# Two-layer retention and attention encoder: the last head's mean square in one full-precision product, attention's output off two banks, gates in pieces

## The chip, the cores and the metric

The kernel runs on one core of a Trainium2 chip. The metric is the time of one execution on the device, in microseconds (us); less is better. The engines are TensorE (PE: matrix products, its weight loads shown as PEld), VectorE (DVE), ScalarE (ACT), GpSimd (POOL) and SyncE (SP, which issues most transfers). Products accumulate in PSUM, in banks; the other working data lie in SBUF.

## The reference

There are 272 tokens (256 and 16 learned ones), 1024 channels and two layers. A layer has a retention branch and a windowed attention branch side by side, merged by sigmoid gates, and then a squared-ReLU MLP.

```python
def retention_branch(q, k, v, gate, log_decay, pad):
    ...
    o = retention_dir(qc, kc, vc, log_decay[0], True) + flip(
        retention_dir(flip(qc), flip(kc), flip(vc), log_decay[1], False))
    o = o.transpose(0, 2, 3, 1, 4).reshape(B, Lp, RET_HEADS, RET_V_DIM)[:, pad:]
    mu = jnp.mean(o, axis=-1, keepdims=True)
    var = jnp.mean(jnp.square(o - mu), axis=-1, keepdims=True)
    o = (o - mu) * lax.rsqrt(var + EPS)
    o = o.reshape(B, L, RET_V).astype(gate.dtype)
    return o * jax.nn.silu(gate)

def reference(...):
    ...
    for l in range(DEPTH):                                   # DEPTH = 2
        u = rms_norm(h, norm_mix_pre[l])
        proj = u @ w_in[l]
        ...
        y_r = retention_branch(...) @ w_ret_o[l]
        y_a = attention_branch(...) @ w_att_o[l]
        mix = (jax.nn.sigmoid(gate_r) * y_r + jax.nn.sigmoid(gate_a) * y_a) @ w_mix_o[l]
        h = h + rms_norm(mix, norm_mix_post[l])
        u = rms_norm(h, norm_ff_pre[l])
        ff = jnp.square(jax.nn.relu(u @ w_ff1[l])) @ w_ff2[l]
        h = h + rms_norm(ff, norm_ff_post[l])
    return h[:, N_META:]
```

The change touches the normalization of retention's output (`rsqrt` of the mean square over a head's 128 channels), the two sigmoid gates, and the product with `w_att_o`.

## The kernel before

Activations lie transposed: 128 channels on the partitions, 272 tokens in the free dimension (256 in the second layer where `c0` is 16). Weights come as units of 128x1024 float32, each split by ACT (line 131, `wh`) and DVE (line 132, `wl`) into a high and a low part in fp32r, in a ring of four; a product is three matmuls per 128 input channels (`mm3`, lines 136 to 138), 24 per unit. PE runs its instructions in one order, and so do ACT and DVE; a scheduler sets these orders from what becomes ready when, within the limits that `tc.issue_after` (not before a named instruction) and `tc.keep_in_program_order` give.

Retention runs head by head (`similar`, `retained`, `normed`, lines 670 to 711). `retained` (line 689) makes a head's output `po` in a bank of tag o (even heads) or t (odd heads), and squares it on ACT; lines 696 and 697 split the square into two fp32r parts `sqs`, one by ACT, one by DVE. `normed` (line 699) takes their mean over the channels by two matmuls against a constant 1/128 (line 702), into a bank of tag t, and then ACT computes Ln (705), Exp with -0.5 (706) and a Square (163), which DVE refines by a Newton step, multiplies by the gate and by `po`, and splits into `rh` and `rl`, the input of the product `ret_o`. Between these steps `fill` puts the products of the units `gate_r` and `gate_a`, so that PE has work while a head's chain runs. The bank tags have 3 (a), 2 (s), 2 (t) and 1 (o) banks; `wide()` (line 85) deals tags a, s and t in turn.

ACT's functions come in sets of tables, and a set is loaded before a function that the present one lacks (ACT_TABLE_LOAD in the rows). Ln and Exp are both in `natural_log_exp_and_others`, Tanh is not. The kernel asks for this set by `preload_act_table_set` at lines 207, 650 and 743; the loads ahead of Tanh (lines 649 and 740) are put in when the program is built, as every load is that the source does not ask for. A sigmoid is computed by Tanh: for `g_r` at line 649, ahead of the heads, and for `gate_r` (`thr`, one instruction) and `gate_a` (`tha`, eight) at lines 740 to 742, held behind the last head's Exp. Then come the product `att_o` (lines 745 to 753), whose result is multiplied with the gate `tha`, `ret_o` (lines 756 to 761), `mix` with the norm behind it (`leave`, line 296, by `mean`, line 180, ten matmuls on zeros, `warm`, line 175, and `rsqrt`, line 186, an Ln, an Exp and a Square on ACT), and the MLP. `leave` runs after the mixer and the first layer's MLP, three times in all; `rsqrt` runs once more at line 378 for each layer's first norm. The last norm (`scaled`, line 834) has an Ln and an Exp for each half of the tokens.

Of the kernel before, what the change touches and what calls it, by code (L numbers as in the profile page):

```python
# [10 lines left out]
F32R = mybir.dt.float32r  # L11
F16 = mybir.dt.float16
BF16 = mybir.dt.bfloat16
AF = mybir.ActivationFunctionType
# [3 lines left out]
P = 128  # L18
# [4 lines left out]
T = SEQ + NM  # L23
# [18 lines left out]
def encoder(ctx: ExitStack, tc: tile.TileContext, order, w, h_in, gains, dec, decm, sink, sinkm, tabs, mats, esel, masks, rel, relm, grow, out):  # L42
    nc = tc.nc
    V, A, PE, G = nc.vector, nc.scalar, nc.tensor, nc.gpsimd
    mul, add, sub, mn = ALU.mult, ALU.add, ALU.subtract, ALU.min

    def pool(name, bufs=1, **kw):
        return ctx.enter_context(tc.tile_pool(name=name, bufs=bufs, **kw))
# [6 lines left out]
    four = pool("four", 4)  # L55
# [5 lines left out]
    def slot(i, name, shape=(KD, T), dt=F32):  # L61
        return big.tile([P] + list(shape), dt, tag=f"b{i}", name=name)
# [4 lines left out]
    def half(i, name):  # L67
        return rows(slot(i, name, (4, T)))

    def tokens(i, name, shape=(KD,), at=32):  # L70
        return slot(i, name, (*shape, ROW), F32R)[..., at:at + T]

    def bank(tag, shape=None):
        t = psum.tile([P, 512], F32, tag=tag, name="ps_" + tag, bufs=BANKS[tag])
        if shape is None:
            return t
        n = int(np.prod(shape))
        v = t[:, :n]
        if len(shape) == 2:
            v = v.rearrange("p (a b) -> p a b", a=shape[0])  # L80
        elif len(shape) == 3:
            v = v.rearrange("p (a b c) -> p a b c", a=shape[0], b=shape[1])
        return v

    def wide():
        turn[0] += 1
        return "asatats"[turn[0] % 7]

    def f(t):
        return t.bitcast(F32)  # L90

    def stt(o, a, s, b, op0=mul, op1=mul):
        V.scalar_tensor_tensor(out=o, in0=a, scalar=s, in1=b, op0=op0, op1=op1)

    def split(xh, xl, x):
        A.activation(xh, x, AF.Copy)  # L96
        V.tensor_tensor(out=xl, in0=x, in1=f(xh), op=sub)  # L97
# [37 lines left out]
    def mm3(ps, ah, al, bh, bl, first=True, last=True):  # L135
        PE.matmul(ps, ah, bh, start=first, stop=False)  # L136
        PE.matmul(ps, ah, bl, start=False, stop=False)  # L137
        return PE.matmul(ps, al, bh, start=False, stop=last)  # L138
# [18 lines left out]
    def proj(x, c0, tag, *name):  # L157
        for _, ps in product(x, c0, tag, *name):
            pass
        return ps  # L160

    def newton(y1, x, e, y, w2):
        sq = A.activation(w2, y, AF.Square)
        if e:
            stt(w2, x, e, w2, op0=add)
        else:
            V.tensor_tensor(out=w2, in0=x, in1=w2, op=mul)
        if y1 is not None:
            stt(y1, w2, 3.0, y, op0=sub)
        return sq  # L170
# [49 lines left out]
    def square(src, c0):  # L220
        sq = two.tile([P, T], F32, tag="sq", name="sq", bufs=3)
        A.activation(sq[:, c0:], src, AF.Square)
        return sq
# [101 lines left out]
    mat = {}  # L325
# [37 lines left out]
    for l in range(DEPTH):  # L363
        c0 = 16 * l
# [5 lines left out]
        if l == 0:  # L370
            mat_sb = load(mats, name="mats")
            mat.update((n, mat_sb[:, i]) for i, n in enumerate(MATS))
            o128 = one.tile([P, P], F32R, tag="o128", name="o128")
# [124 lines left out]
        ao = tokens(5, "ao", (2, 4), 32 - c0)  # L498
# [3 lines left out]
        thr = slot(6, "thr")  # L502
# [46 lines left out]
        def behind():  # L549
            return tc.issue_after(anchor[0])  # L550
# [12 lines left out]
        if l == 0:  # L563
            ps = bank("s")
# [86 lines left out]
        tha = gate["gate_a"] = half("10a", "tha")  # L651
# [16 lines left out]
        sds, pos, pvs = {}, {}, {}  # L668
# [20 lines left out]
        def retained(hh):  # L689
            t = hh // 2  # L690
            po = pos[hh] = bank("ot"[hh % 2], [T])
            for c in range(2):
                PE.matmul(po[:, c0:], vr[:, c, hh * P:(hh + 1) * P], sds[hh][c][:, c0:], start=c == 0, stop=False)
            PE.matmul(po[:, c0:], vm[:, hh], tm[:, t, c0:], start=False, stop=True)
            sq = square(po[:, c0:], c0)
            pvs[hh] = four.tile([P, 2, T], F32R, tag="pt", name="sqs", bufs=3)
            split(*(pvs[hh][:, i, c0:] for i in range(2)), sq[:, c0:])

        def normed(hh):
            pv = bank("t", [T])  # L700
            for i in range(2):
                PE.matmul(pv[:, c0:], o128, pvs[hh][:, i, c0:], start=i == 0, stop=i == 1)
            y = two.tile([P, T], F32, tag="t1", name="vy")
            w2 = two.tile([P, T], F32, tag="t2", name="vw")
            A.activation(y[:, c0:], pv[:, c0:], AF.Ln, bias=eps)
            last = A.activation(y[:, c0:], y[:, c0:], AF.Exp, scale=-0.5)
            newton(w2[:, c0:], pv[:, c0:], 1e-6, y[:, c0:], w2[:, c0:])
            stt(w2[:, c0:], w2[:, c0:], -0.25, gt[:, hh, c0:])
            V.tensor_tensor(out=w2[:, c0:], in0=pos[hh][:, c0:], in1=w2[:, c0:], op=mul)
            split(rh[:, hh, c0:], rl[:, hh, c0:], w2[:, c0:])  # L710
            return last
# [6 lines left out]
        for hh in range(8):  # L718
            with behind():
                if hh < 7:  # L720
                    similar(hh + 1)
                retained(hh)
            fill(F[7])
            if hh == 0:
                for m in range(KD):
                    with tc.issue_after(ready.ins):
                        stt(gt[:, m, c0:], tg[:, m, c0:], 1.0, gt[:, m, c0:], op0=add)
                rh, rl = tokens(7, "rh", at=32 - c0), tokens(8, "rl", at=32 - c0)
            if hh % 2 and hh < 7:
                with behind():  # L730
                    meta((hh + 1) // 2)
            fill(F[6])
            with behind():
                last = normed(hh)
            fill(F[5])
        while queue or current:
            fill(1)

        with tc.issue_after(last.ins):
            A.activation(thr[:, :, c0:], thr[:, :, c0:], AF.Tanh, scale=0.5)  # L740
            for x in tha:
                A.activation(x[:, c0:], x[:, c0:], AF.Tanh, scale=0.5)
        tc.keep_in_program_order(A.preload_act_table_set("natural_log_exp_and_others"))

        for m2 in range(4):
            wh, wl = unit("att_o", m2)
            for i in range(2):
                m = 2 * m2 + i
                ps = bank(wide(), [T])
                for k in range(4):  # L750
                    sl = slice((4 * i + k) * P, (4 * i + k + 1) * P)
                    mm3(ps[:, c0:], wh[:, sl], wl[:, sl], ao[:, 0, k, c0:], ao[:, 1, k, c0:], k == 0, k == 3)
                stt(tha[m][:, c0:], tha[m][:, c0:], 1.0, ps[:, c0:], op0=add)

        z = tokens(2, "zh", at=32 - c0), tokens(3, "zl", at=32 - c0)
        for m in range(KD):
            ps = proj((rh, rl), c0, wide(), "ret_o", m)
# [17 lines left out]
        fs, behind = [], []  # L775
# [8 lines left out]
        for m in range(KF):  # L784
# [4 lines left out]
            ps = proj(u, c0, wide(), "ff1", m)  # L789
# [54 lines left out]
    for j in range(2):  # L844
# [22 lines left out]
        for i in range(2):  # L867
            sl = slice(j * 512, (j + 1) * 512)
# [6 lines left out]
    for i in range(2):  # L875
        for a, b in ((0, 512), (512, 768), (768, 1024)) if i else ((0, 512), (512, 1024)):
            sl = slice(a, b)
# [115 lines left out]
```

## Time and profile before

| what | us |
| --- | --- |
| median of 3 runs (866.87 to 868.93) | 868.81 |
| the profiled execution, its own time | 874.68 |
| its span, first to last instruction | 872.9 |
| PE busy / ACT busy in it | 854.7 / 564.8 |
| first layer's heads in it | 131 to 190 |
| second layer's heads in it | 568 to 624 |

The page gives one profiled execution: busy time per engine, the chain of work that ended last, and groups of instructions with what ended the idle time before them. Times of steps below are from this execution, in us from the start of its span. A row of a timeline has the start, the duration, the engine, the line in the kernel, the operation, what it writes and reads, the size and a count; in brackets stands the engine's idle time before it and what ended it.

### The profile page before, as it was taken

The numbers are of one execution on the slowest core, as the hardware profiler recorded it, in microseconds if no ns is written. First come the engines' busy times: TensorE is split into PE (matmuls) and PEld (weight loads), VectorE is DVE, ScalarE is ACT, GpSimd is POOL, SyncE is SP. The second block draws the span as 40 slices with busy tenths as digits, with TensorE's granted clock in tenths as the row PEclk, the third lists the DMA queues.
The fourth block names the chain that finished last, engine by engine and source line by source line (L and its number), as shares of the span: only waits on it lengthen the run. The fifth ranks groups of instructions, "written<-read, shape, count | busy, mean of one in ns | idle before, by whom it ended". The sixth has DMA issues, their size and how long they took to land.

```text
span 872.9 us, 16696 instructions
## 1 busy us (share of the span) xinstructions
PE 854.7 (98%) x6514; PEld 822.2 (94%) x6514; DVE 608.5 (70%) x1129; ACT 564.8 (65%) x1050; POOL 50.6 (6%) x114
## 2 busy tenths in 40 slices
PE   9999999999999999999999999999999999999997
PEld 8899999999989999999989999999999999998885
DVE  7889888878668555444468898888786775554544
ACT  7448788675558777544455578987845587783432
POOL 2112220000000000000000122200000000000000
PEclk9999999999999999999999999999999999999999
DMA  8544443446545655655635544434376276666661
GB/s 293 194 125 139 122 130 114 145 146 192 164 128 179 190 179 178 176 184 172 178 112 153 162 132 141 141 124 148 115 219 200 90 239 189 183 193 194 190 192 70
DMA packets 41407, 142.15 MB, mean 163 GB/s; under 512 B 5360, under 2 KB 6256, under 8 KB 41328
## 3 DMA queue, kind: packets, MB, share of 16 engines
q1 hardware_dynamic: 40896, 140.43, 52.3%
q8 instruction: 51, 0.84, 0.4%
q10 hardware_dynamic: 432, 0.66, 0.2%
q14 instruction: 28, 0.23, 0.1%
HBM read 140.02 MB, written 1.05 MB: 162 GB/s over the span
## 4 chain that ended last, share of the span: by engine, by line
PE 80%; DVE 10%; ACT 6%; issue 1%; DMA 1%; POOL 0%; SPq 0%; DVEq 0%; ACTq 0%; POOLq 0%
PE ps_a L136 12%; PE ps_a L137 12%; PE ps_a L138 12%; PE ps_s L138 5%; PE ps_s L136 5%; PE ps_s L137 5%; PE ps_t L136 4%; PE ps_t L137 4%; PE ps_t L138 4%; DVE wl L132 3%; PE ps_s L853 2%; PE ps_a L853 2%; PE ps_a L855 2%; PE ps_s L855 2%; PE ps_s L854 2%; PE ps_a L854 2%
## 5 line engine op out<-in xcount | busy, mean ns | idle before, releaser
L132 DVE TENSOR_TENSOR wl<-raw,wh 128x1024 fp32r<-128x1024 f32 x256 | 313.0, 1224 | 199.7 <-ACT wh L131 198.2
L131 ACT ACTIVATE wh<-raw 128x1024 fp32r<-128x1024 f32 x256 | 269.8, 1058 | 204.4 <-PE ps_a L137 62.3
L136 PE MATMUL ps_a<-uh,wh 128*128 128x272 f32 (+1 forms) x912 | 263.0, 289 | 2.8 <-ACT uh L242 2.8
L138 PE MATMUL ps_a<-uh,wl 128*128 128x272 f32 (+1 forms) x912 | 260.0, 285 | 0.5 <-DVE wl L132 0.3
L137 PE MATMUL ps_a<-ul,wh 128*128 128x272 f32 (+1 forms) x912 | 260.1, 286 | 0.0
L136 PEld LDWEIGHTS ps_a<-uh,wh 128*128 128x128 f32 x912 | 172.6, 189 | 3.8 <-ACT uh L242 3.2
L138 PEld LDWEIGHTS ps_a<-uh,wl 128*128 128x128 f32 x912 | 172.9, 190 | 1.2 <-DVE wl L132 0.8
L137 PEld LDWEIGHTS ps_a<-ul,wh 128*128 128x128 f32 x912 | 172.4, 189 | 0.4
L138 PE MATMUL ps_s<-uh,wl 128*128 128x272 f32 (+1 forms) x184 | 52.4, 285 | 0.3 <-DVE wl L132 0.3
L137 PE MATMUL ps_s<-ul,wh 128*128 128x272 f32 (+1 forms) x184 | 52.3, 284 | 0.0
L136 PE MATMUL ps_s<-uh,wh 128*128 128x272 f32 (+1 forms) x184 | 52.2, 284 | 0.0
L136 PE MATMUL ps_t<-uh,wh 128*128 128x272 f32 (+1 forms) x152 | 43.5, 286 | 1.3 <-ACT uh L242 1.3
L137 PE MATMUL ps_t<-ul,wh 128*128 128x272 f32 (+1 forms) x152 | 43.5, 286 | 0.0
L138 PE MATMUL ps_t<-uh,wl 128*128 128x272 f32 (+1 forms) x152 | 43.2, 284 | 0.0
L138 PEld LDWEIGHTS ps_s<-uh,wl 128*128 128x128 f32 x184 | 34.9, 190 | 0.5 <-DVE wl L132 0.5
L136 PEld LDWEIGHTS ps_s<-uh,wh 128*128 128x128 f32 x184 | 34.7, 189 | 0.0
L137 PEld LDWEIGHTS ps_s<-ul,wh 128*128 128x128 f32 x184 | 34.6, 188 | 0.0
L136 PEld LDWEIGHTS ps_t<-uh,wh 128*128 128x128 f32 x152 | 28.6, 188 | 1.5 <-ACT uh L242 1.5
L138 PEld LDWEIGHTS ps_t<-uh,wl 128*128 128x128 f32 x152 | 28.9, 190 | 0.0
L137 PEld LDWEIGHTS ps_t<-ul,wh 128*128 128x128 f32 x152 | 28.6, 188 | 0.1
L97 DVE TENSOR_TENSOR fl<-ft,fh 128x272 fp32r<-128x272 f32 (+1 forms) x64 | 27.6, 433 | 1.0 <-ACT fh L96 0.9
L96 ACT ACTIVATE fh<-ft 128x272 fp32r<-128x272 f32 (+1 forms) x64 | 27.2, 425 | 1.7
(311 smaller groups left out, 1963.5 us busy)
## 6 DMA issues: line engine op xcount, KB each, us to landing
raw<-in_w SPq DMA_DIRECT2D x256, 512.0 KB, 3.7
leads<-in_w SPq DMA_DIRECT2D x6, 256.0 KB, 5.6
tab<-in_tabs SPq DMA_DIRECT2D x2, 544.0 KB, 6.3
h<-in_h_in SPq DMA_DIRECT2D x3, 272.0 KB, 5.8
out<-yt SPq DMA_DIRECT2D x3, 256.0 KB, 2.1
leads<-in_w ACTq DMA_DIRECT2D x2, 256.0 KB, 3.4
gj<-in_grow SPq DMA_DIRECT2D x1, 512.0 KB, 4.7
mats<-in_mats SPq DMA_DIRECT2D x1, 320.0 KB, 7.2
```

The costliest lines, as they stand in the source:

```text
L96: A.activation(xh, x, AF.Copy)
L97: V.tensor_tensor(out=xl, in0=x, in1=f(xh), op=sub)
L131: A.activation(wh[:, c], raw[:, c], AF.Copy)
L132: V.tensor_tensor(out=wl[:, c], in0=raw[:, c], in1=f(wh[:, c]), op=sub)
L136: PE.matmul(ps, ah, bh, start=first, stop=False)
L137: PE.matmul(ps, ah, bl, start=False, stop=False)
L138: return PE.matmul(ps, al, bh, start=False, stop=last)
L853: PE.matmul(pss[i], xh, wh[:, sl], start=kk == 0, stop=False)
L854: PE.matmul(pss[i], xh, wl[:, sl], start=False, stop=False)
L855: PE.matmul(pss[i], xl, wh[:, sl], start=False, stop=kk == KF - 1)
```

## The change

For the last head (7) the square is no longer split: `normed` multiplies it in float32, by one matmul against the float32 matrix of 1/128. This `normed(7)` leaves the loop of the heads and is called by `gates`, behind the second of four steps of `att_o`'s first product; the Tanh of `tha` follows behind its Exp. The Tanh of `thr` becomes three pieces (2, 3 and 3 of its 8 rows), written behind the second, third and fourth unit of `att_o` and held behind nothing. The call of `preload_act_table_set` moves behind all of them. The banks of `att_o` are dealt from tags a and s alone, so that `wide()` is called eight times less in a layer.

```diff
--- before.py
+++ after.py
@@ -693,13 +693,19 @@
                 PE.matmul(po[:, c0:], vr[:, c, hh * P:(hh + 1) * P], sds[hh][c][:, c0:], start=c == 0, stop=False)
             PE.matmul(po[:, c0:], vm[:, hh], tm[:, t, c0:], start=False, stop=True)
             sq = square(po[:, c0:], c0)
-            pvs[hh] = four.tile([P, 2, T], F32R, tag="pt", name="sqs", bufs=3)
-            split(*(pvs[hh][:, i, c0:] for i in range(2)), sq[:, c0:])
+            if hh == 7:
+                pvs[hh] = sq
+            else:
+                pvs[hh] = four.tile([P, 2, T], F32R, tag="pt", name="sqs", bufs=3)
+                split(*(pvs[hh][:, i, c0:] for i in range(2)), sq[:, c0:])
 
         def normed(hh):
             pv = bank("t", [T])
-            for i in range(2):
-                PE.matmul(pv[:, c0:], o128, pvs[hh][:, i, c0:], start=i == 0, stop=i == 1)
+            if hh == 7:
+                PE.matmul(pv[:, c0:], mat["o128"], pvs[hh][:, c0:], start=True, stop=True)
+            else:
+                for i in range(2):
+                    PE.matmul(pv[:, c0:], o128, pvs[hh][:, i, c0:], start=i == 0, stop=i == 1)
             y = two.tile([P, T], F32, tag="t1", name="vy")
             w2 = two.tile([P, T], F32, tag="t2", name="vw")
             A.activation(y[:, c0:], pv[:, c0:], AF.Ln, bias=eps)
@@ -730,27 +736,35 @@
                 with behind():
                     meta((hh + 1) // 2)
             fill(F[6])
-            with behind():
-                last = normed(hh)
+            if hh < 7:
+                with behind():
+                    normed(hh)
             fill(F[5])
         while queue or current:
             fill(1)
 
-        with tc.issue_after(last.ins):
-            A.activation(thr[:, :, c0:], thr[:, :, c0:], AF.Tanh, scale=0.5)
-            for x in tha:
-                A.activation(x[:, c0:], x[:, c0:], AF.Tanh, scale=0.5)
-        tc.keep_in_program_order(A.preload_act_table_set("natural_log_exp_and_others"))
+        def gates(ins):
+            with tc.issue_after(ins.ins):
+                last = normed(7)
+            with tc.issue_after(last.ins):
+                for x in tha:
+                    A.activation(x[:, c0:], x[:, c0:], AF.Tanh, scale=0.5)
 
         for m2 in range(4):
             wh, wl = unit("att_o", m2)
             for i in range(2):
                 m = 2 * m2 + i
-                ps = bank(wide(), [T])
+                ps = bank("asasa"[m % 5], [T])
                 for k in range(4):
                     sl = slice((4 * i + k) * P, (4 * i + k + 1) * P)
-                    mm3(ps[:, c0:], wh[:, sl], wl[:, sl], ao[:, 0, k, c0:], ao[:, 1, k, c0:], k == 0, k == 3)
+                    ins = mm3(ps[:, c0:], wh[:, sl], wl[:, sl], ao[:, 0, k, c0:], ao[:, 1, k, c0:], k == 0, k == 3)
+                    if m == 0 and k == 1:
+                        gates(ins)
                 stt(tha[m][:, c0:], tha[m][:, c0:], 1.0, ps[:, c0:], op0=add)
+            if m2:
+                x = thr[:, (0, 0, 2, 5)[m2]:(0, 2, 5, 8)[m2], c0:]
+                A.activation(x, x, AF.Tanh, scale=0.5)
+        tc.keep_in_program_order(A.preload_act_table_set("natural_log_exp_and_others"))
 
         z = tokens(2, "zh", at=32 - c0), tokens(3, "zl", at=32 - c0)
         for m in range(KD):
```

Line numbers move: line 702 becomes 708 (705 for the last head), 705 and 706 become 711 and 712, 740 becomes 766, 742 becomes 751, 743 becomes 767, and what stands further on (838 and 839 in `scaled`, say) moves by 14.

**ACT, first layer, from the first head's square on.** `sq`, `sqs` are the square and its high part, `tt`, `tb`, `tmx` decays by Exp, `vy` the Ln and the Exp of `normed`, `wh` a unit of weights. Before:

```order
L222 ACTIVATE sq<-ps_o 128x272
L674 ACTIVATE tt<-rel,de 128x256
L96 ACTIVATE sqs<-sq 128x272
L675 ACTIVATE tt<-rel,de 128x144
L705 ACTIVATE vy<-ps_t,eps 128x272
L656 ACTIVATE tmx<-relm,dem 128x272
L706 ACTIVATE vy<-vy 128x272
L676 ACTIVATE tb<-rel,de 128x128
L163 ACTIVATE vw<-vy 128x272
L131 ACTIVATE wh<-raw 128x1024
```

After:

```order
L96 ACTIVATE sqs<-sq 128x272
L675 ACTIVATE tt<-rel,de 128x144
L766 ACT_TABLE_LOAD
L766 ACTIVATE thr<-thr 128x544
L711 ACT_TABLE_LOAD
L711 ACTIVATE vy<-ps_t,eps 128x272
L656 ACT_TABLE_LOAD
L656 ACTIVATE tmx<-relm,dem 128x272
L712 ACTIVATE vy<-vy 128x272
L676 ACTIVATE tb<-rel,de 128x128
L163 ACTIVATE vw<-vy 128x272
L222 ACTIVATE sq<-ps_t 128x272
```

The first piece of `thr`'s Tanh now stands ahead of the first head's Ln, and a load stands before the Tanh, before the Ln and before the next Exp. There are ten loads from here to the Ln of the fifth head, where the load of line 767 stands; the second layer's heads have ten as well, and lack the load of line 649 ahead of them.

**ACT, first layer, at the end of the heads.** Before:

```order
L705 ACTIVATE vy<-ps_t,eps 128x272
L706 ACTIVATE vy<-vy 128x272
L740 ACT_TABLE_LOAD
L740 ACTIVATE thr<-thr 128x2176
L163 ACTIVATE vw<-vy 128x272
L742 ACTIVATE tha<-tha 128x272 x8
L743 ACT_TABLE_LOAD
L96 ACTIVATE rh<-vw 128x272
```

After, the place of the load that the source asks for (at the fifth head), and then the last head's Ln:

```order
L96 ACTIVATE rh<-vw 128x272
L674 ACTIVATE tt<-rel,de 128x256
L675 ACTIVATE tt<-rel,de 128x144
L767 ACT_TABLE_LOAD
L711 ACTIVATE vy<-ps_t,eps 128x272
L656 ACTIVATE tmx<-relm,dem 128x272
L712 ACTIVATE vy<-vy 128x272
```

```order
L711 ACTIVATE vy<-ps_t,eps 128x272
L712 ACTIVATE vy<-vy 128x272
L751 ACT_TABLE_LOAD
L751 ACTIVATE tha<-tha 128x272
L163 ACTIVATE vw<-vy 128x272
L751 ACTIVATE tha<-tha 128x272 x7
```

The load of line 743 stood behind all Tanh; that of line 767 stands ahead of `tha`'s Tanh, before which another load stands, and behind which none that the source asks for follows in this layer.

**ACT, `leave` behind the first layer's mixer.** `yg` is the product times its gain, `y` the Ln and Exp of `rsqrt`. Before:

```order
L222 ACTIVATE sq<-ps_t 128x272
L301 ACTIVATE yg<-ps_t,g 128x272
L189 ACTIVATE y<-ps_o 128x272
L190 ACTIVATE y<-y 128x272
L163 ACTIVATE w_3383<-y 128x272
L131 ACTIVATE wh<-raw 128x1024
```

After:

```order
L222 ACTIVATE sq<-ps_a 128x272
L301 ACTIVATE yg<-ps_a,g 128x272
L189 ACT_TABLE_LOAD
L189 ACTIVATE y<-ps_o 128x272
L190 ACT_TABLE_LOAD
L190 ACTIVATE y<-y 128x272
L163 ACTIVATE w_3381<-y 128x272
L131 ACTIVATE wh<-raw 128x1024
```

A load stands before the Ln and another before the Exp. The same pair stands at the other two calls of `leave`, at `rsqrt` for the second layer's first norm, and at both calls of `scaled`. The first layer's first norm, ahead of all this, has none. In all, the program has 38 loads on ACT, and 9 before.

## Rows read from the trace of the kernel before

**Rows 1.** Page, part 1: busy us of each engine, share of the span, instructions.
```profile
PE 854.7 (98%) x6514; PEld 822.2 (94%) x6514; DVE 608.5 (70%) x1129; ACT 564.8 (65%) x1050; POOL 50.6 (6%) x114
```
**Rows 2.** Page, part 4: the chain that ended last, share of the span by engine.
```profile
PE 80%; DVE 10%; ACT 6%; issue 1%; DMA 1%; POOL 0%; SPq 0%; DVEq 0%; ACTq 0%; POOLq 0%
```
**Rows 3.** Waits of PE, whole span: waiting line, releaser, us in total, times, longest.
```profile
PE ps_a L136 <- ACT uh L242: 2.8, 2, 1.4
...
PE ps_t L136 <- ACT uh L242: 1.3, 1, 1.3
...
PE ps_o L694 <- DVE tm L666: 1.0, 2, 0.8
```
**Rows 4.** Timeline of ACT around 130: start us, us, instruction.
```profile
127.78 1.28 ACT L649 ACT_TABLE_LOAD   x1
129.07 2.03 ACT L649 ACTIVATE tg<-gt 128x2176 f32<-128x2176 f32 x1
131.11 1.28 ACT L650 ACT_TABLE_LOAD   x1
132.40 0.51 ACT L674 ACTIVATE tt<-rel,de 128x256 f32<-128x256 f16 x1
132.82 0.40 ACT L675 ACTIVATE tt<-rel,de 128x144 f32<-128x144 f16 x1
```
**Rows 5.** Windows of retention: length, busy PE PEld DVE ACT POOL, clock, DMA, GB/s.
```profile
137.20:167.20 30.00, 29.84 (x226) 28.91 (x225) 28.64 (x64) 22.20 (x52) 0.00 (x0) 1.00 0.49 143
573.70:602.00 28.30, 28.26 (x227) 27.59 (x226) 27.51 (x61) 21.13 (x48) 0.00 (x0) 1.00 0.48 150
```
**Rows 6.** Timelines of ACT and PE: fifth head of the first layer.
```profile
164.86 0.41 ACT L96 ACTIVATE sqs<-sq 128x272 fp32r<-128x272 f32 x1
...
166.58 0.54 PE L702 MATMUL ps_t<-sqs,o 128*128 128x272 f32 x2
...
167.16 0.49 ACT L705 ACTIVATE vy<-ps_t,eps 128x272 f32<-128x272 f32 x1 [1.18 <-PE ps_t L702]
```
**Rows 7.** Timelines of ACT and PE: `leave` behind the first layer's mixer.
```profile
251.80 0.48 ACT L301 ACTIVATE yg<-ps_t,g 128x272 f32<-128x272 f32 x1
252.72 0.40 ACT L189 ACTIVATE y<-ps_o 128x272 f32<-128x272 f32 x1 [0.44 <-PE ps_o L183]
253.15 0.43 ACT L190 ACTIVATE y<-y 128x272 f32<-128x272 f32 x1
...
256.31 0.39 PE L136 MATMUL ps_a<-uh,wh 128*128 128x272 f32 x1 [1.39 <-ACT uh L242]
```
**Rows 8.** Timelines of ACT, DVE and PE: the second layer's first norm.
```profile
465.93 0.38 ACT L189 ACTIVATE y<-ps_o 128x272 f32<-128x272 f32 x1
...
468.23 0.44 DVE L426 SCALAR_TENSOR_TENSOR vt<-ps_a,rb 128x272 f32<-128x272 f32 x1
...
468.75 0.69 PE L433 MATMUL ps_t<-mats,vt 128*128 128x128 f32 x4
```
**Rows 9.** Timeline of ACT: the end of the program.
```profile
866.96 0.19 ACT L869 ACTIVATION_READ_ACCUMULATOR gj<-ps_a 128x1 f32 x1
...
867.51 0.20 ACT L839 ACTIVATE y<-y 128x1 f32<-128x1 f32 x1
```
**Rows 10.** Windows with pauses of PE, columns as in Rows 5.
```profile
39.90:42.90 3.00, 1.14 (x8) 0.74 (x7) 2.91 (x6) 1.07 (x3) 1.81 (x3) 1.00 0.55 178
42.90:46.50 3.60, 3.60 (x18) 3.60 (x18) 1.36 (x5) 1.06 (x1) 0.00 (x0) 0.53 0.48 148
46.60:50.20 3.60, 3.60 (x31) 3.60 (x31) 2.71 (x7) 1.10 (x2) 0.81 (x3) 1.00 0.49 142
254.90:258.30 3.40, 2.01 (x15) 1.88 (x14) 3.40 (x11) 2.03 (x6) 0.00 (x0) 1.00 0.00 0
```
**Rows 11.** Timeline of PE: last head of the first layer's retention.
```profile
184.02 1.08 PE L693 MATMUL ps_t<-sd,vr 128*128 128x272 f32 x4
...
187.66 0.41 PE L702 MATMUL ps_t<-sqs,o 128*128 128x272 f32 x2
```

## The prediction

> **What bounds the kernel now.** I read the busy times first, then the chain of work that ended last, then PE's waits, and only then the timelines at the places that the change touches. PE is busy 98% of the span, ACT 65% [rows 1]; the chain of work that ended last lies 80% on PE [rows 2]. So PE's queue is the clock of this kernel: what ACT or DVE does is free as long as PE has its operands in time, and what makes PE wait is added in full, because PE has no slack in which to make it up. PE's waits are short and few: the largest are three pauses of 1.3 to 1.4 us behind `leave`, and a wait of 0.8 us for `tm` in the second layer [rows 3]. No wait at all stands at `att_o` or at the last head's `normed`, the place that the change rewrites. The first reading is therefore that there is almost nothing to win there; the question is what the rewritten order costs elsewhere.
>
> **The change part by part.** *The product in float32.* One float32 matmul replaces two fp32r ones. Two float32 products (four records) were busy 1.08 us, and a pair of fp32r ones 0.41 us [rows 11], so PE pays between 0 and 0.2 us a layer; I take 0.1, 0.2 in all. ACT and DVE save one instruction each, beside other work: nothing.
>
> *Banks and the place of the last head.* PE did not wait here before [rows 3], so moving `normed(7)` and taking `att_o` off tag t wins 0. It costs 0 too: a bank is needed again after five products of 12 matmuls, at 0.116 us each (3.6 us for 31 records [rows 10]) some 7 us, while the chain to be waited for, an Ln, an Exp, a load and one Tanh, is some 2.5 us. That cover would fail only if ACT came some 4 us late.
>
> *The loads of tables.* This is where the change bites. A load takes 1.28 us and ACT does nothing else in it: it begins when the instruction ahead has ended (129.07 + 2.03 = 131.10, load at 131.11) and the next begins when the load has ended (131.11 + 1.28 = 132.39, next at 132.40) [rows 4]. Usual instructions overlap: that one, 132.40 + 0.51 = 132.91, was followed at 132.82. So a load amid a full queue costs about 1.4 us, and 1.28 in a chain in which each step waits for the last. The order of the changed kernel has 38 loads instead of 9. Where do the 29 hurt?
>
> 1. *The heads.* Ten loads stand between the first head's square and the fifth head's Ln, in each layer, and the three pieces of Tanh, some 2.1 us together (2.03 us in one piece of the same size [rows 4]): 10 x 1.4 + 2.1 = 16.1 us of new work on ACT. In this stretch ACT was busy 22.20 of 30.00 us in the first layer and 21.13 of 28.30 us in the second, so it had 7.8 and 7.2 us free [rows 5]. The excess is 8.3 and 8.9 us. In the second layer the load of line 649 is gone (its set is already there), 1.3 us earlier for everything behind it: 7.6. PE feels what exceeds its own lead: in the fifth head ACT's half of the square was ready at 164.86 + 0.41 = 165.27, and PE took it at 166.58 [rows 6], 1.3 us later. So PE loses 8.3 - 1.3 = 7.0 and 7.6 - 1.3 = 6.3 us; 13.3 in all. PE has to stand still because its order is fixed: the two matmuls of line 708 wait for `sqs` and behind them queue the gate products that could have run. Weights are not what comes late: `wh` is made some three units ahead. Bounds: if ACT fills its idle time badly, the whole excess goes to PE, 17; if later heads, in which no load stands, give two heads' lead instead of one, 8.
>
> 2. *`leave`, three times.* ACT is done with `yg` at 252.28 and began the Ln at 252.72 [rows 7]. Now a load fills 252.28 to 253.56, the Ln comes 0.84 late; behind its 0.40 us the second load runs 1.28 before the Exp can start. The Exp starts at about 255.27 instead of 253.15: 2.1 us late, and Newton step, update of `h`, `uh` and PE's first matmul (256.31, behind a pause of 1.39 already) are one chain behind it. 3 x 2.1 = 6.4 us, bounds 6 and 6.6. The zeros of `warm` are at their end before, they cover nothing more.
>
> 3. *The second layer's first norm.* The same pair: ACT was busy up to the Ln at 465.93; `vt`, which needs the result, ended at 468.23 + 0.44 = 468.67, and PE took it at 468.75 [rows 8]. No lead, so both loads count: 2.6 us (bound below 1.3, if one fits in ACT's idle time).
>
> 4. *The end.* The last sum is read by 866.96 + 0.19 = 867.15, and the Exp stands at 867.51, right behind its Ln [rows 9]. Two loads come between, 2.5 us on the last chain. The pair for the other half of the tokens falls under the last products.
>
> 5. *The rest*, two loads ahead of `tha`'s Tanh, takes the place of two in the old order: 0.
>
> *The clock.* Longer pauses may cost the clock. After a stretch of 3.0 us in which PE was busy 1.14 us the granted clock went to 0.53 on average, that is mostly the lower level, 1.2 GHz, and in 3.60 us PE got through 18 records instead of 31; at `leave`, where PE was busy 2.01 of 3.40 us, it stayed at 1.00, 2.4 GHz [rows 10]. One fall costs 3.6 - 18 x 0.116 = 1.5 us. The changed kernel's pauses are 1.39 + 2.1 = 3.5 us at three places, 2.6 at one and, for some 2 to 4 us at a time, about three among the heads: seven candidates that lie between the two rows, nearer to the one with the fall. I take three falls, 4.5 us; bounds 0 and 10.5.
>
> *The sum*: 13.3 + 6.4 + 2.6 + 2.5 + 0.2 + 4.5 = 29.5 us. The profiled execution, 874.68, would become 904.2 (its span 872.9 becomes 902.4). The runs shown have a median 5.9 us below the profiled one; on that, 868.8 + 29.5 = **898.3 us**. With all low bounds 8 + 6 + 1.3 + 2.5 = 17.8, 886.6; with all high ones 17 + 6.6 + 2.7 + 2.6 + 0.4 + 10.5 = 39.8, 908.6.
>
> **The rivals.** *A. The heads hide their loads.* ACT's queue may be able to lag by a head without PE noticing, as scores and decays are made a head ahead. Then items 2 to 4 alone remain, 11.5 us: 880.3. For it: ACT has 35% free over the span. Against: `sqs` is needed in the same head, with 1.3 us of lead, against 2.8 us for two loads in each.
>
> *B. Not slower.* The mechanism would be that a load is free where ACT waits anyway, as ahead of the Ln in `leave`; place, the three `leave`s; price, 0; it decides if ACT's wait there is longer than the loads. The wait is 0.44 us [rows 7] against 2.56, and the second load stands behind the Ln, where nothing waits. Were it so throughout, the dropped load of line 649 would leave a gain of the 0.8 us wait for `tm` [rows 3]: 868.0.
>
> *C. Each load costs twice.* If ACT had to empty first and lost as much again as the load lasts, ten loads on the chains (six, two, two) would cost 12.8 us more and twenty in the heads 25.6 more: 936.7. Against: the next instruction began 0.01 us behind a load [rows 4]. The Trainium skill (ScalarE: Activation LUTs, section What ACT_TABLE_LOAD costs) gives 1283 ns for a load and 1380 ns for a drain with every switch, 2.66 us in all; the first figure is what the trace shows, the second it does not show.
>
> *D. More falls of the clock than counted*, with PE's slower products making DVE and ACT wait in their turn: beyond 908, say 913.
>
> The change also doesn't do what it says: the gates' pieces stand among the heads, not in the output stage. That is part of the forecast.
>
> **How the numbers follow.** Forecast (887 to 908): 0.79. A: 0.10, at 880. B: 0.04. C: 0.02. D: 0.05. The range 886 to 908 is the forecast's own, with its bounds; some 0.2 lies outside. About 0.3%, 2.6 us, is what a measurement of this kernel can tell from no change: faster by more than that 0.01, within it 0.03 (the rest of B), slower 0.96.
>
> **What would show it.** Right: 38 loads of 1.28 us; in the first four heads PE waits at line 708 for `sqs` (ACT or DVE), 6 to 7 us in a layer, none at `att_o`; the pauses behind `leave` 3.5 us instead of 1.4; a pause of 2.6 us at line 433 in the second layer; 2.5 us more between the last product and the end; some stretches of granted clock at the lower level behind such pauses. Wrong: no waits at line 708 (A), an Exp at once behind an Ln in `leave` (B), gaps behind the loads (C).

## The result, and the profile after

The changed kernel took 896.81 us, the median of 4 runs (895.70 to 897.53), against 868.76 us for the kernel before in 4 runs (866.87 to 868.93). The ratio is 1.0327, with a 95% interval of 1.0310 to 1.0343; the medians lie 28.0 us apart. The forecast was 898.3 us. The profiled execution of the changed kernel took 896.12 us, with a span of 894.3; that of before lay 5.9 us above its own median, so the two profiles differ by 21.4 us only, and a part of the difference is hidden in them (the last section says where it lies).

The busy times and, in the second row, the shares of the chain that ended last:

```profile
PE 856.7 (96%) x6514; PEld 822.2 (92%) x6514; DVE 609.0 (68%) x1127; ACT 599.4 (67%) x1081; POOL 52.5 (6%) x114
...
PE 73%; ACT 13%; DVE 10%; issue 2%; DMA 1%; POOL 0%; SPq 0%; DVEq 0%; ACTq 0%; POOLq 0%
```

Beside [rows 1, 2]: ACT has 31 instructions more, of which 29 are loads, and is busy 34.6 us longer; ACT's share of the last chain went from 6% to 13%, and PE's from 80% to 73%. PE is busy about as long as before. What was added stands between its matmuls. PE's waits show where (waiting line, releaser, us in total, times, longest):

```profile
PE ps_t L136 <- ACT uh L242: 7.0, 2, 3.5
PE ps_t L708 <- ACT sqs L96: 5.7, 4, 2.1
PE ps_a L136 <- ACT uh L242: 3.5, 1, 3.5
PE ps_t L433 <- DVE vt L426: 2.8, 2, 2.2
PE ps_t L708 <- DVE vw L93: 2.6, 1, 2.6
PE ps_t L708 <- DVE sqs L97: 1.1, 2, 0.9
```

The waits for `uh` were 2.8 + 1.3 = 4.1 us [rows 3] and are 10.5. Those at line 708, the mean of squares of a head, are new: 5.7 + 2.6 + 1.1 = 9.4 us. The wait for `tm` [rows 3] is gone, with the load of line 649 in the second layer.

*Among the heads*, ACT's timeline from the first head's square on (start, us, instruction):

```profile
136.26 1.28 ACT L766 ACT_TABLE_LOAD   x1
137.56 0.66 ACT L766 ACTIVATE thr<-thr 128x544 f32<-128x544 f32 x1
138.24 1.28 ACT L711 ACT_TABLE_LOAD   x1
139.53 0.49 ACT L711 ACTIVATE vy<-ps_t,eps 128x272 f32<-128x272 f32 x1
140.04 1.28 ACT L656 ACT_TABLE_LOAD   x1
141.34 0.52 ACT L656 ACTIVATE tmx<-relm,dem 128x272 f32<-128x272 f16 x1
```

From 136.26 to 141.86, 5.6 us, ACT does two short instructions of its old work, one piece of the Tanh and three loads. The next instruction stands 0.01 to 0.02 us behind each load, as in [rows 4]. The windows that answer to [rows 5] (length, busy PE PEld DVE ACT POOL, clock, DMA, GB/s) run from the first load to the load ahead of the fifth head's Ln in the first layer, and over the first eight of the ten loads in the second. Behind them stands one of the four matmuls of the first layer that waited:

```profile
136.20:172.80 36.60, 33.13 (x229) 30.99 (x227) 28.40 (x62) 35.46 (x63) 0.00 (x0) 0.95 0.38 116
585.50:615.50 30.00, 27.07 (x212) 25.86 (x211) 23.33 (x53) 29.57 (x53) 0.00 (x0) 1.00 0.33 106
```

```profile
154.08 0.39 PE L708 MATMUL ps_t<-sqs,o 128*128 128x272 f32 x1 [2.08 <-ACT sqs L96]
```

ACT, at 22.20 of 30.00 us before, is busy 35.46 of 36.60 us: here it, and not PE, sets the pace (in the second layer it is busy 29.57 of 30.00 us), and PE stands still for 3.5 us of this stretch.

*In `leave`*, the pair of loads and what PE then waits, beside [rows 7]:

```profile
256.45 0.48 ACT L301 ACTIVATE yg<-ps_a,g 128x272 f32<-128x272 f32 x1
256.95 1.28 ACT L189 ACT_TABLE_LOAD   x1
258.25 0.40 ACT L189 ACTIVATE y<-ps_o 128x272 f32<-128x272 f32 x1
258.66 1.28 ACT L190 ACT_TABLE_LOAD   x1
259.95 0.43 ACT L190 ACTIVATE y<-y 128x272 f32<-128x272 f32 x1
```

```profile
263.11 0.39 PE L136 MATMUL ps_t<-uh,wh 128*128 128x272 f32 x1 [3.54 <-ACT uh L242]
```

The Exp starts 3.50 us behind `yg` and not 1.35, and PE's pause is 3.54 us and not 1.39. The other two are 3.54 and 3.43 us.

*At the end*, the sum is read, then load, Ln, load, Exp, beside [rows 9]:

```profile
885.94 0.19 ACT L883 ACTIVATION_READ_ACCUMULATOR gj<-ps_a 128x1 f32 x1
886.15 1.28 ACT L852 ACT_TABLE_LOAD   x1
887.45 0.29 ACT L852 ACTIVATE y<-ysum,ex 128x1 f32<-128x1 f32 x1
887.76 1.28 ACT L853 ACT_TABLE_LOAD   x1
889.05 0.20 ACT L853 ACTIVATE y<-y 128x1 f32<-128x1 f32 x1
```

The Exp stands 889.05 - 886.13 = 2.92 us behind the sum, and stood 0.36 behind it: 2.56 us on the last chain.

### The profile page after: what moved, and what is told of

It reads as the page before. It is cut to its first block, busy times and chain, and to the rows that moved or that the text cites. A ratio compares the mean times of both kernels' runs of the same rounds, so it can differ in the third digit from the quotient of the medians.

```text
span 894.3 us, 16731 instructions
## 1 busy us (share of the span) xinstructions
PE 856.7 (96%) x6514; PEld 822.2 (92%) x6514; DVE 609.0 (68%) x1127; ACT 599.4 (67%) x1081; POOL 52.5 (6%) x114
## 4 chain that ended last, share of the span: by engine, by line
PE 73%; ACT 13%; DVE 10%; issue 2%; DMA 1%; POOL 0%; SPq 0%; DVEq 0%; ACTq 0%; POOLq 0%
PE ps_a L136 11%; PE ps_a L137 11%; PE ps_a L138 11%; PE ps_s L137 4%; PE ps_s L136 4%; PE ps_s L138 4%; PE ps_t L136 4%; PE ps_t L137 4%; PE ps_t L138 4%; DVE wl L132 3%; ACT wh L131 2%; PE ps_a L868 2%; PE ps_a L867 2%; PE ps_a L869 2%; ACT L711 1%
## 5 line engine op out<-in xcount | busy, mean ns | idle before, releaser
L136 PE MATMUL ps_t<-uh,wh 128*128 128x272 f32 (+1 forms) x168 | 48.0, 288 | 7.0 <-ACT uh L242 7.0
L137 PE MATMUL ps_s<-ul,wh 128*128 128x272 f32 (+1 forms) x176 | 50.3, 286 | 0.0
L138 PE MATMUL ps_s<-uh,wl 128*128 128x272 f32 (+1 forms) x176 | 49.8, 283 | 0.0
L137 PE MATMUL ps_t<-ul,wh 128*128 128x272 f32 (+1 forms) x168 | 48.3, 287 | 0.0
L138 PE MATMUL ps_t<-uh,wl 128*128 128x272 f32 (+1 forms) x168 | 48.1, 286 | 0.0
L136 PEld LDWEIGHTS ps_t<-uh,wh 128*128 128x128 f32 x168 | 32.4, 194 | 7.4 <-ACT uh L242 7.4
L138 PE MATMUL ps_a<-fh,wl 128*128 128x272 f32 x128 | 36.7, 287 | 0.0
L136 PE MATMUL ps_a<-fh,wh 128*128 128x272 f32 x128 | 36.7, 287 | 0.0
L137 PE MATMUL ps_a<-fl,wh 128*128 128x272 f32 x128 | 36.7, 287 | 0.0
L137 PEld LDWEIGHTS ps_t<-ul,wh 128*128 128x128 f32 x168 | 32.3, 193 | 0.0
```

## The experiments

The theory: all of the loss is the 29 loads, in two independent shares. One is ten loads among the heads of each layer, where ACT runs full; the other is the pairs at Ln and Exp, which have no combined set to find because the load that the source asks for now stands too early. PE's longer pauses also cost clock. The rivals: that the rewritten output stage itself costs (or wins) something, that the heads hide their loads (A), and that a fall of the clock is no cost of its own. Where a result below is given in us, it is the ratio less one, times the median of before on the same chip.

**The three pieces held back.** The pieces of `thr`'s Tanh wait for the last head's Exp, so that the loads return to 9; all else of the change stays.

```diff
+        held7 = []
...
+            held7[:] = [last.ins]
...
-                A.activation(x, x, AF.Tanh, scale=0.5)
+                with tc.issue_after(held7[0]):
+                    A.activation(x, x, AF.Tanh, scale=0.5)
```

> The changed kernel with one difference: the three pieces of the gate's Tanh are held behind the last head's Exp, so that they stand with the other gate's Tanh and the load that the source asks for stands behind all of them. The program then has 9 table loads, as the kernel before; the float32 product, its place inside the output stage and the banks are those of the change. Loads theory (they are all of the loss): 868.8 plus 0 to 1, so within 0.3% of before. Rival, the other parts of the change cost too (late last head, fewer banks): over 872, and PE waits at the output stage. Rival, the other parts win what the loads hid: under 866.

869.60 us against 869.88 (12 and 17 runs): 0.9999, 0.9980 to 1.0019. Full precision, banks and the last head's place are worth nothing that can be measured, and no wait at `att_o` or at line 705 stands in the trace, as none stood there before. So the loss comes with the place of the three pieces and with the loads that this place brings.

**The heads alone.** The pieces stay free among the heads, but a second request for the combined set is placed behind `tha`'s Tanh, so that no pair is left: 29 loads.

```diff
-                    A.activation(x[:, c0:], x[:, c0:], AF.Tanh, scale=0.5)
+                    done[:] = [A.activation(x[:, c0:], x[:, c0:], AF.Tanh, scale=0.5).ins]
...
         tc.keep_in_program_order(A.preload_act_table_set("natural_log_exp_and_others"))
+        with tc.issue_after(done[0]):
+            A.preload_act_table_set("natural_log_exp_and_others")
```

> The changed kernel with a second request for the Ln and Exp set behind the last Tanh: the ten loads among each layer's heads stay, the pairs in leave, the second layer's first norm and the end are gone (29 loads). Loads theory with the balance of ACT's idle time: 7.0 and 7.6 us for the heads (the load of line 649 is back in the second layer), 0.2 for the product and one or two falls of the clock of 1.5: 885 to 887. Rival A (heads hide their loads): 869. Rival, a load costs its 1.28 us in full wherever it stands: 20 more loads, 25.6 us, 894.

882.82 us, 1.0161 (1.0138 to 1.0185): 14.0 us. Rival A is out. The waits at line 708 are those of the changed kernel, and the waits for `uh` are back at 2.7 + 1.4 us:

```profile
PE ps_t L708 <- ACT sqs L96: 5.6, 4, 2.1
PE ps_t L708 <- DVE vw L93: 2.6, 1, 2.6
```

How the heads grow is seen in windows from their first product (`ps_s<-qk,qkl`) to the first matmul of `att_o`, in each layer. First the kernel with the pieces held, then this one (columns as above):

```profile
129.37:190.97 61.60, 61.29 (x465) 59.38 (x463) 52.49 (x114) 44.24 (x89) 0.00 (x0) 1.00 0.45 138
564.88:623.49 58.61, 57.66 (x465) 56.21 (x464) 51.23 (x112) 43.24 (x84) 0.00 (x0) 1.00 0.47 143
```

```profile
129.41:197.87 68.46, 64.15 (x464) 61.12 (x463) 52.89 (x114) 58.82 (x102) 0.00 (x0) 0.98 0.41 124
571.73:636.76 65.03, 58.73 (x464) 56.32 (x463) 51.27 (x112) 57.38 (x97) 0.00 (x0) 1.00 0.41 129
```

The heads grow by 6.9 and 6.4 us, 13.3 in all. PE's idle time grows from 0.3 to 4.3 us in the first layer, and PE is busy 2.9 us longer, with a mean clock of 0.98: one fall lies in the window. In the second layer the idle time grows from 0.95 to 6.3 us at an unbroken clock, and the busy time by 1.1, which no run here explains. The time lies below the 885 to 887 us expected: the second layer's heads grew by 6.4 us and not by 7.6, and the 6.9 us of the first already hold its fall of the clock.

**The pairs alone.** The kernel before, without the line that asks for the combined set: six pairs' loads, none among the heads; 18 loads.

```diff
-        tc.keep_in_program_order(A.preload_act_table_set("natural_log_exp_and_others"))
```

> The kernel before without the request of line 743: the heads are untouched, and the pairs of loads stand in leave, the second layer's first norm and the end as in the changed kernel (18 loads). Loads theory: 6.4 + 2.6 + 2.5 less 0.8 to 1.3 for the load of line 649 that falls away in the second layer, plus two to four falls of the clock of 1.5 us behind the longer pauses: 882 to 886. Rival B (a load where ACT waits anyway is free): 868. Rival, the clock does not fall or costs nothing: 879.5.

885.46 us, 1.0187 (1.0158 to 1.0216): 16.3 us, from an edit that holds nothing else of the change. The waits are those of the changed kernel, without line 708 (line 433 has 2.8 us again):

```profile
PE ps_a L136 <- ACT uh L242: 7.1, 2, 3.5
PE ps_t L136 <- ACT uh L242: 3.4, 1, 3.4
```

Heads and pairs together make 14.0 + 16.3 = 30.3 us, and the changed kernel lost 28.4 by its ratio. The two shares add, within their intervals.

**The pauses in `leave` filled.** The changed kernel with 22 of the zero matmuls of `warm` instead of 10; they are no part of the result.

```diff
-        warm(10)
+        warm(22)
```

> The changed kernel with 22 instead of 10 matmuls on zeros in leave, which fill the pause of 3.5 us there but for some 0.6; loads unchanged (38). Clock theory: the three falls behind leave are gone, 1.0 to 1.5 us each: 892 to 894. Rival, the slower clock behind leave lies beside PE's wait for uh and costs nothing: 896.8.

894.04 us, 1.0284 (1.0261 to 1.0308), against 1.0327 for the changed kernel: 24.7 us instead of 28.4. PE still waits 0.9 us behind its zeros, and the clock stays. The stretch behind the first `leave` in the changed kernel, and the same here:

```profile
259.60:263.10 3.50, 0.00 (x0) 0.00 (x0) 2.63 (x7) 2.72 (x6) 0.00 (x0) 1.00 0.00 0
263.10:267.10 4.00, 3.99 (x21) 3.98 (x22) 4.00 (x12) 2.37 (x6) 0.00 (x0) 0.65 0.00 0
267.10:271.10 4.00, 4.00 (x32) 4.00 (x31) 4.00 (x10) 1.46 (x3) 0.00 (x0) 0.93 0.00 0
```

```profile
261.00:265.00 4.00, 3.52 (x32) 3.33 (x30) 2.25 (x6) 3.22 (x5) 0.00 (x0) 1.00 0.00 0
265.00:269.00 4.00, 3.62 (x26) 3.47 (x27) 4.00 (x12) 2.75 (x7) 0.00 (x0) 1.00 0.00 0
```

In the changed kernel the pause is empty, and 21 records follow in 4 us at a mean clock of 0.65, that is partly at 1.2 GHz. With zeros in the pause the clock holds 2.4 GHz. All three falls behind `leave` are gone, and in this profile the one among the second layer's heads is gone too, which the added zeros don't touch. The gain, 3.7 us by the ratios, is uncertain by some 2.5 us, so two further runs asked for the price of a fall.

**One piece among the heads.** Only the first piece stays free, with a request for the combined set right behind it; the others wait for `tha`'s Tanh. 19 loads, six among the first layer's heads and four among the second's.

```diff
-                A.activation(x, x, AF.Tanh, scale=0.5)
+                with tc.issue_after(done[0]) if m2 > 1 else ExitStack():
+                    A.activation(x, x, AF.Tanh, scale=0.5)
+                if m2 == 1:
+                    tc.keep_in_program_order(A.preload_act_table_set("natural_log_exp_and_others"))
```

> The changed kernel with the first piece of the gate's Tanh left among the heads, the Ln and Exp set asked for behind it, the other two pieces held behind the last gate's Tanh, and the set asked for again behind them. Six loads among the first layer's heads and four among the second's, instead of ten each; none in leave or at the end (19 in all). Balance theory (a layer loses what the new work on ACT exceeds its idle time and PE's lead by): 6 x 1.4 + 0.7 = 9.1 against some 4 us of idle time and 1.3 of lead, 3 to 4 us, and 6.3 against 2.5 and 1.3, 2 to 3 us, a fall of the clock at most: 874 to 877. Rival, every load costs its 1.28: 10 x 1.28, 882. Rival, a threshold (fewer than ten are hidden): 869 to 870.

879.29 us against 871.36: 1.0090 (1.0062 to 1.0118), 7.8 us. The kernel before was 2.6 us above its usual median on this chip, so the absolute numbers of the expectation were missed, and the ratio is to be read. One row of PE's waits holds the effect:

```profile
PE ps_t L708 <- ACT sqs L96: 4.0, 2, 2.4
```

Four us of waits against 9.3, and 7.8 us of loss against 14.0: fewer loads, a smaller loss, but the first ones are not free. The heads of the two layers, in the same windows as above:

```profile
128.81:195.65 66.84, 63.86 (x465) 61.15 (x463) 52.93 (x114) 52.72 (x96) 0.00 (x0) 0.97 0.41 127
568.93:629.42 60.49, 57.92 (x464) 56.02 (x463) 51.40 (x112) 48.77 (x89) 0.00 (x0) 1.00 0.45 138
```

Against 61.60 and 58.61 us they grow by 5.2, with a fall of the clock in it, and by 1.9. The balance had 3 to 4 and a fall, and 2 to 3. Ten loads at their full 1.28 us would be 12.8 us, and that lies outside the interval (5.4 to 10.3 us).

**The pieces free in the first layer only.** The kernel of the heads alone, with this:

```diff
-                A.activation(x, x, AF.Tanh, scale=0.5)
+                with tc.issue_after(done[0]) if l else ExitStack():
+                    A.activation(x, x, AF.Tanh, scale=0.5)
```

> The kernel of the run with the heads alone, its three pieces of Tanh free in the first layer only and held behind the last gate's Tanh in the second: ten loads among the first layer's heads, none among the second's (19 in all). Its trace showed 4.0 us of waits at line 708 and a fall of the clock in the first layer, 5.3 us of waits in the second. Theory: the first layer's 5.5 us alone: 874 to 876. Rival, the layers share a cost elsewhere (the two don't add): near 869 or near 883.

879.79 us, 1.0088 (1.0060 to 1.0115): 7.7 us, about half of the 14.0 with both layers, and more than the 5.5 expected, though within the interval (5.2 to 10.0). Waits at line 708 of 2.9 + 1.1 us, all in the first layer, and the heads of both layers in the same windows as above:

```profile
PE ps_t L708 <- ACT sqs L96: 2.9, 2, 2.1
...
PE ps_t L708 <- DVE sqs L97: 1.1, 2, 0.9
```

```profile
127.83:196.46 68.63, 64.32 (x465) 61.20 (x463) 52.86 (x114) 58.81 (x102) 0.00 (x0) 0.98 0.39 124
570.03:628.55 58.52, 57.58 (x464) 56.05 (x463) 51.15 (x112) 43.23 (x84) 0.00 (x0) 1.00 0.48 143
```

The first layer's heads grow by 7.0 us, the second's not at all. The expectation had added the waits and one fall, 4.0 + 1.5; PE loses more than that, since it is busy 3.0 us longer (64.32 against 61.29). Each layer thus pays for its own heads, as the balance of ACT's time in each wants it.

**The pairs, with the pauses filled.** The kernel of the pairs alone, with more zeros; they are no part of the result here either.

```diff
-        warm(10)
+        warm(22)
```

> The kernel before without the request of line 743 (pairs of loads in leave, the second layer's first norm and the end), and with 22 instead of 10 matmuls on zeros in leave. Clock theory: the three falls behind leave, seen in the run with 10, are gone: 3 less than that run's 885.5, 881.5 to 883.5. Rival, those falls cost nothing since PE waits for uh there: 885.5.

881.99 us, 1.0119 (1.0083 to 1.0156), against 1.0187 without the added zeros. In the trace the falls behind `leave` are gone, and one, behind the second layer's first norm, is left. The gain, 5.9 us of ratio, agrees with three falls of 1.5 us within the intervals, but also with more.

**The price of a fall by itself.** The kernel before, without the ten zero matmuls in `leave`, which are no part of the result. No load moves.

```diff
-        warm(10)
```

> The kernel before without the ten matmuls on zeros in leave (they are no part of the result). The chain of ACT and DVE behind which PE waits there is untouched, so PE's pause grows from 1.4 to some 3.8 us at three places and costs nothing by itself; only the clock can cost. Clock theory: it falls behind each, as in the changed kernel, and PE's slower matmuls cost 1 to 1.5 us each: 2.5 to 4.5 us more than before, 872 to 874 where before is 869.5. Rival, a fall costs nothing net (PE waits for uh there, or its pace is better after a pause): 868 to 870.

874.61 us against 869.77 (12 and 17 runs): 1.0053 (1.0035 to 1.0071), 4.6 us. The pauses are now 3.6 us, since nothing fills them:

```profile
256.06 0.60 PE L136 MATMUL ps_a<-uh,wh 128*128 128x272 f32 x1 [3.62 <-ACT uh L242]
```

```profile
252.50:256.50 4.00, 0.44 (x2) 0.44 (x3) 3.07 (x9) 3.03 (x6) 0.00 (x0) 0.82 0.22 88
256.50:260.50 4.00, 4.00 (x19) 4.00 (x19) 4.00 (x12) 2.29 (x6) 0.00 (x0) 0.50 0.00 0
260.50:264.50 4.00, 4.00 (x29) 4.00 (x28) 4.00 (x10) 1.32 (x4) 0.00 (x0) 0.82 0.00 0
```

The first matmul does not come later than before (256.06 against 256.31 [rows 7]), so an emptier pause cost nothing; the products behind it ran at 1.2 GHz. Three such places, 4.6 us: 1.5 us for a fall in the mean, and the rival on the clock is out. This fall is longer than the one behind `leave` in the changed kernel: there the two windows behind the pause have a mean clock of 0.65 and 0.93, here the three from the pause on have 0.82, 0.50 and 0.82. So a fall of the changed kernel need not cost as much.

No kernel here is faster than the one before; the best of them, with the pieces held, equals it.

## Why the prediction was right, step by step

The time was forecast as 898.3 us and came out 1.5 us below that, in the middle of the range. The steps by their size; where nothing else is said, what was measured is the length of that stretch in the changed kernel less its length in the kernel with the pieces held:

| step | forecast us | measured us |
|---|---|---|
| product in float32, banks, place of the last head | 0.2 | -0.1, interval -1.7 to 1.7 (the run with the pieces held) |
| heads, first layer | 7.0 | 68.60 - 61.60 = 7.0, a fall of the clock in it |
| heads, second layer | 6.3 | 64.21 - 58.61 = 5.6 (with 22 zeros, without a fall) |
| `leave`, three pauses | 6.4 | 10.5 - 4.1 = 6.4 |
| second layer's first norm | 2.6 | 2.2 |
| the end | 2.5 | 2.6 |
| falls of the clock | 3 x 1.5 = 4.5 | 1.1 + 0.5 + 1.3 + 1.3 + 0.7 = 4.9 |

The measured column makes 28.6 us with its own -0.1, and the medians differ by 28.0. The column takes chosen stretches of single profiles; the two profiles as a whole differ by 896.12 - 871.82 = 24.3 us. Most of the rest is in two places: the kernel with the pieces held has a fall of the clock at 43 us, which the other lacks (its heads begin 1.7 us later), and between the second layer's heads and the pause of `leave` it ran at the slower pace of the last section (2.5 us).

*Product, banks, place of the last head.* Right: nothing won and nothing lost.

*The heads.* The mechanism was right: ACT's time adds up. The rows are those from the first head's square to the fifth head's Ln in the first layer, before and in the changed kernel:

```profile
135.83:167.16 31.33, 31.17 (x237) 30.24 (x236) 30.01 (x67) 23.53 (x56) 0.00 (x0) 1.00 0.47 137
```

```profile
134.87:174.10 39.23, 35.06 (x244) 32.92 (x243) 30.93 (x68) 38.07 (x69) 0.00 (x0) 0.96 0.37 109
```

ACT was busy 14.5 us longer, its idle time went from 7.8 to 1.2 us, and the stretch grew by 7.9 us. The excess was put at 8.3. In the second layer (572.39 to 602.04 before, 585.58 to 622.54 behind the change) ACT was busy 14.0 us longer, 6.7 us of idle time went, and the stretch grew by 7.3, against 8.9. So the new work was less than the 16.1 us of the sum and ACT's idle time was not quite used up, and PE's heads grew by 0.9 us less than ACT's stretch in the first layer, where a lead of 1.3 had been taken off. That the first layer comes out at 7.0 exactly is therefore in part luck, all the more as the measured 7.0 holds a fall that the sum counts elsewhere.

In the windows the waits of PE at line 708 sum up to 4.0 and 5.4 us: "6 to 7 us in a layer" was too much for the waits alone, since a part of the growth is PE being slower behind its pauses. Nor do they stand in the first four heads only: the first layer's are at the first, third and fifth head, the second layer's at the second, third and fifth. The second layer in the changed kernel, with and without a fall (the run with 22 zeros has none here), tells what the fall is worth there:

```profile
579.37:644.87 65.50, 59.96 (x464) 57.75 (x463) 51.34 (x112) 56.25 (x96) 0.00 (x0) 0.97 0.41 128
```

```profile
580.86:645.07 64.21, 58.65 (x465) 56.50 (x464) 51.28 (x112) 56.26 (x96) 0.00 (x0) 1.00 0.43 130
```

PE stands still for 5.5 us in both and is busy 1.3 us longer in the first. For the first layer this can't be split: every kernel here with the pieces free in it has a fall there, at 155 us.

*A wait that was not foreseen.* The longest of the second layer, 2.58 us at 621.38, is not for the new `sqs`: the matmul needs a bank of tag t back, and that is held until the fourth head's `vw` is out, at 620.82 + 0.42 = 621.24 us. Its cause is the same, since ACT's queue runs late: ACT's half of the new `sqs` was ready at 620.92, 0.3 us earlier, so without the bank the wait would have been about as long.

*`leave`, first norm, end.* Right to 0.4 us each. In each, two loads stand in a chain with nothing beside it, and the sum was made of rows of the kernel before alone.

*The clock.* Here the count failed, and the term came out right by two errors that offset. Three falls were taken; the trace shows six: one among the heads of each layer, one behind each `leave`, and one behind the second layer's first norm. Five of them have a price of their own: in order of time 1.1, 0.5, 1.3, 1.3 and 0.7 us. The first is the way from the first to the second matmul behind a `leave`, 461.91 - 263.11 = 198.80 us against 195.52 with the pieces held, less the pause's growth of 2.15; the others are read in the same manner, the fourth against the run with 22 zeros. None reaches 1.5 us. The prediction took that price from 18 records against the 31 of unbroken work [rows 10]; behind a `leave` PE does fewer than that at the full clock too. With the pieces held, the first two stretches of 4 us behind the first `leave` are

```profile
255.95:259.95 4.00, 4.00 (x29) 3.85 (x30) 4.00 (x12) 2.37 (x6) 0.00 (x0) 1.00 0.00 0
259.95:263.95 4.00, 4.00 (x34) 4.00 (x33) 4.00 (x10) 1.46 (x3) 0.00 (x0) 1.00 0.00 0
```

and the changed kernel does 21 and 32 records in them: ten less, 1.2 us at 0.116 us each. The mean of 1.5 us in the last experiment is that of longer falls. The fall at 43 us in the profile of before [rows 10] is missing from that of after; kernels here have or lack it without a connection to their edits that I can see, so its absence is not counted as a gain.

*The level.* The prediction took off 5.9 us because the profile of before lay above its median. That was needed: 874.68 + 28.0 would have been 902.7.

*The rivals.* A fell with the heads alone (14.0 us, not 0). B fell with the pairs alone: the load that stands where ACT had waited for 0.44 us puts the Ln 258.25 - 256.45 = 1.80 us behind the start of `yg` instead of 0.92, so that 0.44 us of its 1.28 were free and not more. Its one true part is the load of line 649 with the wait for `tm`: in the kernel of the pairs alone, which lacks both, the second layer's heads took 629.13 - 571.55 = 57.6 us against 58.6. C: the next instruction stands 0.01 to 0.02 us behind a load in every place shown. The Trainium skill (ScalarE: Activation LUTs, section What ACT_TABLE_LOAD costs) adds a drain of 1380 ns to each switch, and no run here shows it. D: the falls were more than counted, but each was cheaper.

*A reading that was wrong without weight.* The wait of 0.8 us for `tm` is not among the largest of PE behind those in `leave`: three of 0.9 to 1.0 us, for `idle`, `pads` and `vt`, stand in the first 100 us of the profile of before. The change touches none of them.

## What to carry to other kernels

Count the table loads in the order of the built program before a function of another set is moved or cut in pieces: each piece that a scheduler lets drift among Ln and Exp brings up to three loads, and a request for a combined set serves only what stands behind it. To price them, add ACT's new work to its busy time in that very stretch; what exceeds the stretch, less the lead that PE's operands have, is about the loss, whatever the average over the span says. A pause of PE is to be priced twice, by its length and, where the granted clock falls behind it, by the slower products that follow.

## What was not expected of the hardware

In these profiles PE's matmuls have two paces, some 3.5% apart, at the same granted clock of 1.00. Both rows are of the same code, the second layer's first feed-forward products; the first is of the kernel with the pieces held, the second of that with the pieces free in the first layer only:

```profile
735.00:755.00 20.00, 20.00 (x179) 20.00 (x178) 11.88 (x16) 15.66 (x30) 0.00 (x0) 1.00 0.66 196
```

```profile
735.00:755.00 20.00, 20.00 (x173) 20.00 (x172) 11.18 (x14) 15.38 (x29) 0.00 (x0) 1.00 0.63 186
```

PE is busy throughout and does 179 or 173 records in 20 us; both profiles have 6514 records in all, so none is missing from one alone. The pace differs between executions and can change within one: the kernel with the pieces held does 173 records in the 20 us from 643.49 and 179 in those from 703.49. The profile of before ran at the lower pace here (172 records), and the changed kernel's at the higher (178); that, with the fall at 43 us, is why their profiles differ by 21.4 us where the medians differ by 28.0. From the first matmul of `att_o` to the first behind `leave` in each layer, and from the second layer's to the last product, the changed kernel took 66.82, 61.86 and 178.06 us, and the kernel before 65.80, 61.65 and 180.52; less the longer pauses (2.15 us each in the first two) and the fall (0.7 us in the third) some 6 us are gained by pace. The pace is also why the heads cost 13.3 us at `att_o` in the kernel with the heads alone while its span grew by 10.8 only: behind that point it ran 179 records in 20 us where the other had 173. What sets the pace is open; no run here was made for it.
